# Tree attention on one core: three stores and three layings moved in GpSimd's program, and K of heads 32 to 47 read in rows of sixteen nodes

## The chip, the core and the metric

The kernel runs on one core of a Trainium2 chip. The core has a matrix engine (TensorE, called PE in the profile, with its weight loads as PEld), a vector engine (VectorE, DVE), an activation engine (ScalarE, ACT), a general engine (GpSimd, POOL) and a synchronising engine (SyncE, SP). Each works through its own list of instructions in order and waits where an instruction needs something that is not there yet. Sixteen DMA engines move data between the memory outside (HBM) and the memory on the core (SBUF). Matrix products are written to a third memory, PSUM.

The metric is the device time of one execution in microseconds. The kernel before takes 132.79 us, the median of 3 runs that lay between 132.54 and 132.94.

## The reference

Q, K and V hold 8 x 12 = 96 heads with 512 nodes of 64 numbers each, in float32. The 512 nodes are a binary tree in heap order: the parent of node i is (i - 1) // 2. A node attends to itself and its ancestors only.

```python
mask[i, i] = 1
parent = i
while parent > 0:
    parent = (parent - 1) // 2
    mask[i, parent] = 1
...
scores = np.einsum('bhqd,bhkd->bhqk', Q, K) * scale
scores = scores + (1 - mask) * (-1e9)
weights = np.exp(scores - np.max(scores, axis=-1, keepdims=True))
weights = weights / (np.sum(weights, axis=-1, keepdims=True) + 1e-10)
return np.einsum('bhqk,bhkd->bhqd', weights, V).astype(np.float32)
```

## The kernel before

**Work.** The 96 heads are worked through in 48 pairs. A loop over i from 0 to 48 holds, at step i, some of four parts, in an order that a string of letters gives:

- S, the scores of pair i. `scores1` multiplies the top 128 nodes of the tree, as keys, with all queries; `scores2` does the rest. Both first multiply two small code matrices (`codes`, `far`), whose product is a large negative number wherever the mask forbids. ACT takes the exponential out of PSUM (tile `s`) into SBUF (tile `e`).
- V, the products of pair i - 1: `values` multiplies `e` with the values `vt` into the PSUM tile `ob`, and `norm` lets DVE take the reciprocal of the sums (`rec`, line 733) and scale the result into the output tile `of` (line 735). There is one `ob`, so the next pair's V waits for this scaling.
- K and Q, a turn of keys or queries of later pairs. They lie in SBUF with nodes on the partitions, and PE transposes them into PSUM (`ktp`, `qtp`), from where DVE copies them to where the scores read them (`kq` or `kk` for keys, `qq` for queries). One turn covers two pairs.

**Three layouts.** A load puts 4, 8 or 16 neighbouring nodes of a head in one row of a partition, so a row read from HBM is 1, 2 or 4 KB long (the load converts float32 to bf16 on its way). Pairs below `WIDE` = 8 have rows of four nodes. Queries of pairs from `FAR` = 16 on have rows of sixteen, keys only from `KFAR` = 24 on. In a turn of keys, `wide_k` (rows of eight) has three DVE copies into `kq`, lines 482, 486 and 490, and serves its own two pairs. `far_k` (rows of sixteen) has three copies into `kk`, two at line 521 and one at 525; the turns work on groups of four pairs, and only both turns together complete the keys of their group. So the keys of pairs 16 to 19 are then needed whole before S of pair 16.

**Lists of values.** V needs its values in three tiles `vt`, which there are twice; 16 heads share one set. POOL, DVE and ACT copy pieces of the loaded rows `vst` there (line 374). Which piece goes to which engine at which step is a fixed table (`BY_VECTOR`, `BY_SCALAR`, `STEADY_VECTOR`, and POOL's own program). DVE's last piece for heads 32 to 47, called C0, is copied at step 16, and V of pair 16 (at step 17) needs it.

**POOL's program.** `pool_program` is one list, in the order in which POOL works through it. It holds nearly every load and store (issuing one takes POOL 0.6 to 0.95 us), POOL's pieces of the values (`spread_top`: four pieces of 16 heads' top nodes; `spread_pool`: named pieces) and four copies `lay_beside` (line 448). A laying copies a loaded tile of the last sixteen heads so that the two heads of a pair lie beside each other, and the turns of the pairs 40 to 47 read that copy. POOL works strictly in this order. Before it issues a load or store it waits until the one eight places earlier in its queue has landed, so eight are under way at most. All of them go through one queue (q0 in the profile), in order of issue.

**The order around the change.** Up to head 55 the loads stand in a written list. From head 56 on a loop over blocks of eight heads appends: K, Q, what remains of V, and a store of eight heads as soon as it lies `BEHIND` = 56 heads behind the load. The remaining stores follow, with the layings between them. Stores of the last heads go through the queues of SP and ACT.

```python
WIDE, FAR, KFAR = 8, 16, 24
...
if i >= max(FAR, KFAR - 4):
    steps = ("SVK", "SVQ", "SVK", "SQV")[i % 4]
elif i == FAR - 1:
    steps = "SQVK"
```

Of the kernel before, what the change touches and what calls it, by code (L numbers as in the profile page):

```python
# [10 lines left out]
CODE = 2048.0  # L11
CODE_ROWS = 40
NOUT = 20
BEHIND = 56

# [104 lines left out]
def kernel(  # L120
# [7 lines left out]
    nc = tc.nc  # L128
# [4 lines left out]
    NH = B * H  # L133
    NQ = NH // 4
    NP = 2 * NQ
    WIDE, FAR, KFAR = 8, 16, 24
    KB, VB = 8, 16
    assert NH % VB == 0

# [611 lines left out]
    APART, APART_AT, APART_ROWS = 72, 38, 116  # L751
# [7 lines left out]
    def pool_program():  # L759

        ops = [
            (load_k, 2, 2), (load_q, 2, 2), (load_v, 0, 4), (load_v, 4, 4),
            (load_k, 4, 2), (load_k, 6, 2), (load_q, 4, 2), (load_k, 8, 4),
            (load_q, 6, 2), (load_q, 8, 4), (load_v, 8, 8), (load_k, 12, 4),
            (load_q, 12, 4), (load_k, 16, 4), (load_rows, 1, "upper"),
            (load_q, 16, 4), (load_rows, 1, "even"), (load_k, 20, 4), (load_rows, 1, "odd"),
            (load_q, 20, 4), (load_k, 24, 8), (load_q, 24, 4), (load_rows, 2, "upper"),
            (load_q, 28, 4), (load_rows, 2, "leaves0", "leaves1"), (load_k, 32, 8), (load_q, 32, 8),
            (load_rows, 3, "upper"),
            (spread_pool, (1, "Z0", 8, 16), (1, "Z1", 8, 16), (1, 6, 8, 16), (1, 9, 8, 16)),  # L770
            (load_q, 40, 8), (load_k, 40, 8), (load_rows, 3, "leaves0", "leaves1"), (load_k, 48, 8),
            (spread_top, 2), (spread_pool, (2, "Z0", 0, 16), (2, "Z1", 0, 16)), (load_q, 48, 8),
            (spread_pool, (2, "X", 0, 16), (2, "M", 0, 16), (2, "D1", 0, 16)), (spread_top, 3, 0, 12),
            (load_rows, 4, "upper"), (spread_top, 3, 12, 16),
        ]
        loaded, stored = 72, 0
        for h in range(56, NH, KB):
            top = [(spread_top, h // VB + 0)] if h % VB == 8 and 4 <= h // VB + 0 < NH // VB else []
            if top:
                top.append((spread_pool, (h // VB, "Z0", 0, 16), (h // VB, "Z1", 0, 16)))  # L780
            ops += [(load_k, h, KB)] + top + [(load_q, h, KB)]
            if h == 64:
                ops.append((
                    spread_pool, *[(3, part, 0, 16) for part in ("Z0", "Z1", "X", "M", "D1")]
                ))
            while loaded < min(h + 32, NH):
                names = ("leaves0", "leaves1") if loaded % VB else ("upper",)
                ops.append((load_rows, loaded // VB) + names)
                loaded += KB
            if top:  # L790
                o = h // VB
                ops.append((spread_pool, *[(o, part, 0, 16) for part in ("X", "M", "D1")]))
# [4 lines left out]
        while stored < NH - KB:  # L797
            n = 2 if stored == APART else 0
            ops.append((store, nc.gpsimd, stored + n, KB - n))
            if stored == 40:  # L800
                ops.append((lay_beside, "qst", 80 // KB))
            if stored == 64:
                ops += [(lay_beside, "kst", 88 // KB), (lay_beside, "qst", 88 // KB)]
            stored += KB
        ops += [(store, nc.gpsimd, NH - KB + h, 2) for h in (0, 4)]
        return ops

# [165 lines left out]
```

## Time and profile before

| | |
|---|---|
| median of 3 runs | 132.79 us (132.54 to 132.94) |
| the profiled execution's own time | 132.49 us |
| its span, from first to last instruction | 130.7 us |
| busy share of the span | PE 87%, DVE 81%, ACT 77%, POOL 65% |
| granted TensorE clock, mean | 0.986 of full speed |
| read from HBM, written to it | 37.94 MB, 12.58 MB |

The profiled execution is 0.30 us below the median and lies 1.8 us above its span. Times of the trace are counted from the start of the span. A row of the timeline names the start, the busy time, engine, line, operation and tiles with the number of instructions that it merges, and in square brackets how long the engine had been idle before, and what ended that. Issue rows (DMA_DIRECT2D) are the time that POOL spends on issuing, not the transfer's. The figure GB/s counts bytes on the side that is written; a load reads float32 and writes bf16, so it reads twice that from HBM.

### The profile page before, as it was taken

Reading aid. Unit: us, or ns where it says so; the run is one execution under the profiler, and the core shown is the slowest. Engines: PE = TensorE matmul, PEld = TensorE weight load, DVE = VectorE, ACT = ScalarE, POOL = GpSimd, SP = SyncE. Lnnn points to the kernel's source line nnn. Section 1 sums busy time; section 2 is a strip of 40 time slices with the busy share of each in tenths; the row PEclk is TensorE's granted clock in tenths of the full one; section 3 lists DMA queues with packets and bytes.
Section 4 is the critical chain, followed back from the end, with each engine's and each line's share of the span. In section 5 each row is a group of like instructions: output and inputs, shape, how many; then the busy total and the mean of one; then the engine's idle time right before and its main releaser. Section 6 shows DMA issues by size and latency. Waiting matters only on the chain.

```text
span 130.7 us, 5436 instructions
## 1 busy us (share of the span) xinstructions
PE 113.7 (87%) x2353; PEld 81.0 (62%) x2353; DVE 105.6 (81%) x254; ACT 101.1 (77%) x163; POOL 84.4 (65%) x116
## 2 busy tenths in 40 slices
PE   6688969999799887899998999896999997999940
PEld 2354755766577566677776786674677675776630
DVE  3349779888999998989998998987898997894560
ACT  4179676989779995968987799797689785889930
POOL 6999625354483999995299899953999963202130
PEclk9999999999999999999999999999999999999995
DMA  2999999999999999999999999999999999999984
GB/s 89 248 190 192 201 195 201 201 202 205 201 203 208 208 205 207 208 210 205 207 211 201 283 292 210 270 309 231 338 228 322 257 277 397 402 404 386 382 339 145
DMA packets 26071, 32.25 MB, mean 247 GB/s; under 512 B 1240, under 2 KB 19544, under 8 KB 26048
## 3 DMA queue, kind: packets, MB, share of 16 engines
q0 software_dynamic: 24384, 30.41, 111.4%
q1 hardware_dynamic: 944, 0.91, 2.2%
q10 hardware_dynamic: 720, 0.59, 1.5%
q8 instruction: 18, 0.29, 0.8%
q14 instruction: 5, 0.04, 0.1%
HBM read 37.94 MB, written 12.58 MB: 386 GB/s over the span
## 4 chain that ended last, share of the span: by engine, by line
DVE 29%; DMA 28%; PE 22%; POOL 7%; ACT 6%; issue 4%; ACTq 0%; DVEq 0%; POOLq 0%
DMA vst<-in_V_dram 17%; DMA qst<-in_Q_dram 11%; DVE of L735 9%; PE ob L696 8%; DVE vt L374 6%; PE s L601 3%; DVE qq L577 3%; ACT e L652 3%; DVE rec L733 3%; DVE kk L521 3%; POOL kst L247 2%; PE s L608 2%; DVE kk L525 2%; POOL qst L247 2%; ACT e L618 2%
## 5 line engine op out<-in xcount | busy, mean ns | idle before, releaser
L618 ACT ACTIVATE e<-s 128x1024 bf16<-128x1024 f32 x40 | 40.9, 1024 | 15.0 <-PE s L608 14.6
L696 PE MATMUL ob<-vt,e 128*128 128x65 bf16 (+1 forms) x940 | 37.1, 197 | 2.6 <-DVE of L735 1.0
L696 PEld LDWEIGHTS <-e 128*128 128x128 bf16 (+1 forms) x960 | 30.1, 102 | 9.6 <-DVE of L735 1.9
L374 POOL COPY vt<-vst 32x512 int32<-32x512 int32 (+4 forms) x44 | 32.5, 739 | 4.7 <-PE ob L696 2.5
L652 ACT ACTIVATE e<-s 128x384 bf16<-128x384 f32 x80 | 34.7, 490 | 0.0
L735 DVE TENSOR_TENSOR of<-ob,rec 128x512 f32<-128x512 f32 x47 | 32.5, 691 | 1.6
L374 DVE COPY vt<-vst 32x1024 bf16<-32x1024 bf16 (+5 forms) x47 | 20.9, 445 | 2.8 <-DMA vst<-in_V_dram 1.9
L743 POOL DMA_DIRECT2D out_dram<-of x13 | 11.5, 888 | 12.9 <-DVE of L735 12.4
L733 DVE RECIPROCAL rec<-ob 128x8 f32<-128x8 f32 x47 | 9.5, 202 | 9.9 <-PE ob L696 9.3
L257 POOL DMA_DIRECT2D kst<-in_K_dram x11 | 8.0, 725 | 7.4 <-DMA qst<-in_Q_dram 3.2
L601 PE MATMUL s<-far,codes 40*128 40x512 bf16 x64 | 12.5, 386 | 0.0
L635 PEld LDWEIGHTS <-codes 40*128 40x128 bf16 x80 | 6.2, 94 | 8.7 <-issue 3.9
L614 ACT ACTIVATE e<-s 128x1024 bf16<-128x1024 f32 x8 | 8.2, 1023 | 4.1 <-PE s L608 4.0
L577 DVE COPY qq<-qtp 128x1024 bf16<-128x1024 bf16 x16 | 10.9, 680 | 0.3 <-PE qtp L572 0.3
L635 PE MATMUL s<-far,codes 40*128 40x384 bf16 x64 | 10.7, 324 | 0.4 <-ACT e L652 0.2
L257 POOL DMA_DIRECT2D qst<-in_Q_dram x12 | 8.5, 708 | 3.8 <-DMA vst<-in_V_dram 1.9
L374 ACT COPY vt<-vst 32x512 int32<-32x512 int32 (+3 forms) x19 | 10.4, 545 | 0.4
L608 PE MATMUL s<-qq,kk 64*128 64x512 bf16 x48 | 9.2, 378 | 1.0 <-DVE qq L577 1.0
L646 PEld LDWEIGHTS <-kk 64*128 64x128 bf16 x192 | 8.4, 94 | 2.6
L521 DVE COPY kk<-ktp 128x256 bf16<-128x256 bf16 x24 | 9.0, 414 | 0.7 <-PE ktp L513 0.7
L302 POOL DMA_DIRECT2D vst<-in_V_dram x7 | 5.6, 800 | 6.0 <-DMA vst<-in_V_dram 4.3
L572 PE MATMUL qtp<-ptile,qst 128*64 128x128 bf16 x192 | 7.5, 221 | 1.7 <-DVE qq L577 1.0
(64 smaller groups left out, 178.2 us busy)
## 6 DMA issues: line engine op xcount, KB each, us to landing
out_dram<-of POOLq DMA_DIRECT2D x10, 1024.0 KB, 15.2
kst<-in_K_dram POOLq DMA_DIRECT2D x9, 512.0 KB, 16.5
qst<-in_Q_dram POOLq DMA_DIRECT2D x8, 512.0 KB, 14.8
vst<-in_V_dram POOLq DMA_DIRECT2D x12, 256.0 KB, 13.5
vst<-in_V_dram POOLq DMA_DIRECT2D x6, 512.0 KB, 12.9
qst<-in_Q_dram POOLq DMA_DIRECT2D x6, 256.0 KB, 12.1
kst<-in_K_dram POOLq DMA_DIRECT2D x4, 256.0 KB, 10.3
out_dram<-of POOLq DMA_DIRECT2D x1, 768.0 KB, 13.0
```

The source lines that it names most:

```text
L257: return nc.gpsimd.dma_start(out=kept[b][:, h0 % KB:h0 % KB + n, :, :].rearrange("p (g x) t d -> p g (x t d)", x=x), in_=src[:, h0 // x:(h ...
L374: return copy(out=dst, in_=src)
L521: nc.vector.tensor_copy(out=columns(flat, 32 * unit, (640, 4), (step, 2), (4, 8), (1, 4)), in_=columns(kp, base, (256, 4), (128, 2), (1, 8 ...
L577: nc.vector.tensor_copy(out=qqs[j][:, :, 8 * last:8 * last + 8, :].rearrange("p b u c -> p b (u c)"), in_=quarters,)
L601: nc.tensor.matmul(out=sp[:, a, :], lhsT=(k1code if i < WIDE else k1wide)[64 * a:64 * a + CODE_ROWS, :], rhs=(q1code, q1wide, q1far)[(i >= ...
L608: nc.tensor.matmul(out=sp[:, a, :], lhsT=keys(i, a, TOP), rhs=qTs[i][64 * a:64 * a + 64, :, :].rearrange("p t c -> p (t c)"), start=False, ...
L618: ) if i < WIDE else nc.scalar.activation(
L635: nc.tensor.matmul(out=flat[:, a, :, :].rearrange("p u (t c) -> p u t c", t=4)[:, :, :, 32 // n:], lhsT=k2wide[64 * a:64 * a + CODE_ROWS, ...
L652: nc.scalar.activation(out=e2s[i % NE][:, a, :, 32:128].rearrange("p t (r u) -> p t r u", u=n), in_=flat[:, a, :, :].rearrange("p u (t r) ...
L696: nc.tensor.matmul(out=ob[lo:hi, a, 65 * t:65 * t + 65], lhsT=e[:, a, PLACE[t], lo:hi], rhs=vt[vtile[tile_v][0]][:, head(i, a) % VB, vtile ...
L733: nc.vector.reciprocal(out=rec[:, a:a + n, :, :], in_=o4[:, a:a + n, :, D:D + 1])
L735: nc.vector.tensor_tensor(out=ofs[j][:, h0:h1 + 1:head(i, 1) - head(i, 0), :, :], in0=o4[:, a:a + n, :, 0:D], in1=rec[:, a:a + n, :, :].to ...
```

## The change

**POOL's program from head 56 on is written out.** Read against the order before:

- the stores of heads 8 to 15, 16 to 23 and 24 to 31 each stand behind one more block of loads. Before, they stood ahead of K of heads 72, 80 and 88; now they stand behind Q of these heads and, for 72 and 88, behind the pieces of values that go with that block;
- the load of V's upper rows for heads 80 to 95 stands behind K and Q of heads 64 to 71 and the pieces that follow them, where it stood ahead of the first store;
- the layings: Q of heads 80 to 87 is laid right after K of these heads, ahead of the stores of heads 24 and 32 (it stood behind the stores of heads 32 and 40); K and Q of heads 88 to 95 are laid ahead of the stores of heads 40 to 71 (they stood behind them).

POOL's queue before, from the load of V's leaf rows for heads 80 to 95 (`vst`, 32x8x512) to Q of heads 80 to 87; `kst` and `qst` are loads of K and Q, `out_dram` is a store, each of eight heads:

```order
L293 DMA vst<-in_V_dram 32x8x512 x2
L743 DMA out_dram<-of 128x8x256
L257 DMA kst<-in_K_dram 128x2x1024
L374 COPY vt_0_115<-vst 32x16x32 x4
L374 COPY vt_1_116<-vst 32x32x32 x2
L257 DMA qst<-in_Q_dram 128x2x1024
L374 COPY vt_2_117<-vst 32x32x32 x2
L374 COPY vt_1_116<-vst 32x8x2x32
L743 DMA out_dram<-of 128x8x256
L257 DMA kst<-in_K_dram 128x2x1024
L257 DMA qst<-in_Q_dram 128x2x1024
```

The same place now:

```order
L292 DMA vst<-in_V_dram 32x8x512 x2
L301 DMA vst<-in_V_dram 64x16x256
L256 DMA kst<-in_K_dram 128x2x1024
L373 COPY vt_0_115<-vst 32x16x32 x4
L373 COPY vt_1_116<-vst 32x32x32 x2
L256 DMA qst<-in_Q_dram 128x2x1024
L373 COPY vt_2_117<-vst 32x32x32 x2
L373 COPY vt_1_116<-vst 32x8x2x32
L742 DMA out_dram<-of 128x8x256
L256 DMA kst<-in_K_dram 128x2x1024
L256 DMA qst<-in_Q_dram 128x2x1024
```

The store that stood ahead of K of heads 72 to 79 (the first `kst` here), that of heads 8 to 15, is now behind the pieces that follow Q of these heads; the upper rows of V (`vst`, 64x16x256) have come in ahead of that K.

POOL's queue before, from the last pieces of values to the end of the layings (L448, `kst<-kst` and `qst<-qst`):

```order
L374 COPY vt_1_122<-vst 32x8x2x32
L448 COPY kst<-kst 128x1024
L743 DMA out_dram<-of 128x8x256 x2
L448 COPY qst<-qst 128x1024
L743 DMA out_dram<-of 128x8x256 x3
L448 COPY kst<-kst 128x1024
L448 COPY qst<-qst 128x1024
L743 DMA out_dram<-of 128x6x256
```

The same place now:

```order
L373 COPY vt_1_122<-vst 32x8x2x32
L447 COPY kst<-kst 128x1024
L447 COPY qst<-qst 128x1024
L742 DMA out_dram<-of 128x8x256 x2
L447 COPY kst<-kst 128x1024
L447 COPY qst<-qst 128x1024
L742 DMA out_dram<-of 128x8x256 x4
L742 DMA out_dram<-of 128x6x256
```

The layings have moved ahead of stores; the first laying stands where it stood, right behind the last pieces.

**K of heads 32 to 47 in rows of sixteen nodes.** `KFAR` falls from 24 to 16, so the keys of pairs 16 to 23 are loaded and turned as those from pair 24 on were: two loads of eight heads change their shape, and four turns become `far_k`. The turns of keys move to even steps (14, 16, 18) where they stood on 15, 17 and 19, those of queries to odd ones; with that, K of heads 40 to 47 is loaded ahead of Q of these heads.

DVE's queue before, from the copies of the keys' turn at step 15 (`kq`) on; `rec` and `of` are the two operations of a pair's scaling, `qq` a turn of queries, `vt_2_123` and `vt_1_116` pieces of values:

```order
L482 COPY kq<-ktp 128x2x128
L486 COPY kq<-ktp 128x4x64
L490 COPY kq<-ktp 128x4x2x64
L374 COPY vt_2_117<-vst 32x8x2x64
L733 RECIPROCAL rec<-ob 128x8
L735 TENSOR_TENSOR of<-ob,rec 128x2x256
L577 COPY qq<-qtp 128x4x256
L374 COPY vt_1_116<-vst 32x8x2x64
L733 RECIPROCAL rec<-ob 128x8
L735 TENSOR_TENSOR of<-ob,rec 128x2x256
L482 COPY kq<-ktp 128x2x128
```

The same place now, from the queries' turn at step 15 (`qq`) on:

```order
L576 COPY qq<-qtp 128x4x256
L732 RECIPROCAL rec<-ob 128x8
L734 TENSOR_TENSOR of<-ob,rec 128x2x256
L373 COPY vt_2_117<-vst 32x8x2x64
L732 RECIPROCAL rec<-ob 128x8
L734 TENSOR_TENSOR of<-ob,rec 128x2x256
L520 COPY kk<-ktp 128x4x2x32
L520 COPY kk<-ktp 128x8x32
L524 COPY kk<-ktp 128x8x64
L373 COPY vt_1_116<-vst 32x8x2x64
L732 RECIPROCAL rec<-ob 128x8
```

At step 16 the turn that stands between the scaling and the piece C0 (`vt_1_116`) was one of queries, with one copy; it is now one of keys, with three.

The diff:

```diff
-    WIDE, FAR, KFAR = 8, 16, 24
+    WIDE, FAR, KFAR = 8, 16, 16
...
-            (load_q, 40, 8), (load_k, 40, 8), (load_rows, 3, "leaves0", "leaves1"), (load_k, 48, 8),
+            (load_k, 40, 8), (load_q, 40, 8), (load_rows, 3, "leaves0", "leaves1"), (load_k, 48, 8),
...
-            if stored + KB + BEHIND <= h + KB:
-                ops.append((store, nc.gpsimd, stored, KB))
-                stored += KB
-        ops.insert(-1, (lay_beside, "kst", 80 // KB))
...
+        ops += k7 + q7 + leaves(4) + out(0)
+        ops += k8 + q8 + [(spread_pool, *[(3, part, 0, 16) for part in ("Z0", "Z1", "X", "M", "D1")])]
+        ops += leaves(5) + [(load_rows, 5, "upper")]
+        ops += k9 + tops(4) + q9 + rest(4) + out(8)
+        ops += k10 + q10 + out(16)
+        ops += k11 + tops(5) + q11 + rest(5)
+        ops += [(lay_beside, "kst", 80 // KB), (lay_beside, "qst", 80 // KB)] + out(24) + out(32)
+        ops += [(lay_beside, "kst", 88 // KB), (lay_beside, "qst", 88 // KB)]
+        for h in range(40, NH - KB, KB):
+            n = 2 if h == APART else 0
+            ops += out(h + n, KB - n)
...
         if i >= max(FAR, KFAR - 4):
             steps = ("SVK", "SVQ", "SVK", "SQV")[i % 4]
+        elif i == FAR - 2:
+            steps = "SQVK"
         elif i == FAR - 1:
-            steps = "SQVK"
+            steps = "SQV"
```

In it `k8` and `q8` load K and Q of heads 64 to 71 (the digit is the block of eight heads), `tops(o)` and `rest(o)` are POOL's pieces of the sixteen heads from 16 o on, `leaves(o)` loads their leaf rows of V, and `out(h)` stores eight heads from h on.

More of the change, by code (lines that the diff above doesn't have):

```diff
@@ L13 @@
 NOUT = 20
-BEHIND = 56
 UNITS = (
@@ L775, in pool_program @@
         ]
[L776 to L792, printed above, removed]
-            if stored + KB + BEHIND <= h + KB:
-                ops.append((store, nc.gpsimd, stored, KB))
-                stored += KB
@@ L796, in pool_program, with tops @@
-        ops.insert(-1, (lay_beside, "kst", 80 // KB))
[L797 to L804, printed above, removed]
+        def tops(o):
+            return [(spread_top, o), (spread_pool, (o, "Z0", 0, 16), (o, "Z1", 0, 16))]
```

13 lines of the change are left out of this document (added).

## The prediction

> **What bounds the kernel.** I read the page first, then PE's timeline with the idle time in brackets, then POOL's, DVE's, and the windows of the end.
>
> ```profile
> PE 113.7 (87%) x2353; PEld 81.0 (62%) x2353; DVE 105.6 (81%) x254; ACT 101.1 (77%) x163; POOL 84.4 (65%) x116
> DMA  2999999999999999999999999999999999999984
> GB/s 89 248 190 192 201 195 201 201 202 205 201 203 208 208 205 207 208 210 205 207 211 201 283 292 210 270 309 231 338 228 322 257 277 397 402 404 386 382 339 145
> ```
>
> No engine is full, but the DMA engines are at 90% or more from the second slice to the 38th. The 200 GB/s of the first half are loads, 400 GB/s read; stores reach 400 at the end. So the DMA queue is a second bound beside compute, and the order within it decides when each load lands.
>
> PE, from 70 us to the end, where it stood idle:
>
> ```profile
> 70.36 0.39 PE L608 MATMUL s<-qq,kk 64*128 64x512 bf16 x2 [0.35 <-DVE qq L577]
> 80.91 0.64 PE L513 MATMUL ktp<-ptile,kst 128*64 128x128 bf16 x16 [0.23 <-DMA kst<-in_K_dram]
> 83.62 0.64 PE L572 MATMUL qtp<-ptile,qst 128*64 128x128 bf16 x16 [0.45 <-DMA qst<-in_Q_dram]
> 91.38 0.64 PE L513 MATMUL ktp<-ptile,kst 128*64 128x128 bf16 x16 [0.98 <-DMA kst<-in_K_dram]
> 93.87 0.64 PE L572 MATMUL qtp<-ptile,qst 128*64 128x128 bf16 x16 [0.23 <-DMA qst<-in_Q_dram]
> 108.66 0.39 PE L608 MATMUL s<-qq,kk 64*128 64x512 bf16 x2 [0.60 <-DVE qq L577]
> ```
>
> Four waits for loads, K and Q of heads 64 to 71 and of 72 to 79: 0.23 + 0.45 + 0.98 + 0.23 = 1.89 us. Behind 94 us no load is waited for any more, and the chain of waits runs through PE and DVE to the last scaling. The end:
>
> ```profile
> 126.55 0.42 DVE L735 TENSOR_TENSOR of<-s,rec 128x256 f32<-128x256 f32 x1
> 115.00:120.00 5.00, 4.76 (x87) 3.22 (x85) 4.01 (x9) 4.18 (x8) 0.00 (x0) 1.00 1.03 402
> 120.00:125.00 5.00, 4.81 (x104) 3.35 (x98) 2.05 (x6) 4.81 (x9) 1.87 (x3) 1.00 0.94 369
> 125.00:127.00 2.00, 0.75 (x16) 0.52 (x14) 1.76 (x5) 0.18 (x1) 0.45 (x1) 1.00 0.88 350
> 127.00:129.00 2.00, 0.00 (x0) 0.00 (x0) 0.00 (x0) 0.00 (x0) 0.00 (x0) 0.54 0.88 271
> 129.00:130.70 1.70, 0.00 (x0) 0.00 (x0) 0.00 (x0) 0.00 (x0) 0.00 (x0) 0.50 0.12 39
> ```
>
> The last number is GB/s. Compute ends at 126.97, the last bytes come some 2.4 us later, and in the last ten us the DMA engines are no longer full: 5 x 369 + 2 x 350 + 2 x 271 + 1.7 x 39 = 3,150 KB, which at the 402 of the row above take 7.8 us, where they took about 9.2 (the last window is busy for 0.2). So an earlier end of compute shortens the run one to one, up to about 1.3 us; beyond that the queue bounds it.
>
> **The moved stores and the moved load of V (a gain).** The price of a transfer in the queue: the K and Q loads that PE waited for at 91.38 and 93.87 landed 2.49 us apart, one load of eight heads. In POOL's rows the next K is there at 98.93:
>
> ```profile
> 90.23 4.87 POOL L374 COPY vt<-vst 32x512 int32<-32x512 int32 x6 [2.49 <-PE ob L696]
> 95.05 0.70 POOL L257 DMA_DIRECT2D qst<-in_Q_dram  x1
> 95.79 2.95 POOL L374 COPY vt<-vst 32x1024 int32<-32x1024 int32 x3
> 98.93 1.04 POOL L448 COPY kst<-kst 128x1024 int32<-128x1024 int32 x1 [0.19 <-DMA kst<-in_K_dram]
> 101.70 1.05 POOL L448 COPY qst<-qst 128x1024 int32<-128x1024 int32 x1
> 106.43 1.04 POOL L448 COPY kst<-kst 128x1024 int32<-128x1024 int32 x1 [0.89 <-DMA kst<-in_K_dram]
> 108.91 1.04 POOL L448 COPY qst<-qst 128x1024 int32<-128x1024 int32 x1 [1.43 <-DMA qst<-in_Q_dram]
> ```
>
> From 93.87 to 98.93 one store and that K passed: 5.06 - 2.49 = 2.57 us for a store of eight heads. K and Q of heads 64 to 71 have the upper rows of V ahead of them no more (as many bytes read as a K load: 2.5 us earlier). Those of heads 72 to 79 have these rows again, but no store of heads 8 to 15: 2.6 us earlier. Those of 80 to 87 and 88 to 95 likewise, by one store each. Each lead exceeds its wait (0.98 at most), so all four waits go: -1.89 us. Bounds: 0, if the loads land no earlier, and -1.89. I take the whole, since in the page's slices the DMA engines have no hole before 124 us. Issuing does not hold the loads back: each waits for a landing eight places earlier, and one transfer less is ahead. The stores themselves have nobody waiting but their ten output tiles, of which the first is needed again at step 40. The queue ends with one store more behind the last load; the bytes are the same.
>
> **The layings.** Those of Q 80 to 87 and of K and Q 88 to 95 now hold up the stores behind them in POOL. Laying Q 88 to 95 waits for the last load, in the worst case until 108.91 as now, so the stores of heads 40 to 71, which are now issued ahead of it, come from about 107.5 on (the load lands 2.6 us earlier). The queue holds two stores behind that load, 2 x 2.57 = 5.1 us of cover, against 1.05 for the laying and 0.9 for an issue: 0. Without that cover it would cost about 2 us. The stores of heads 74 to 95 wait for DVE as before. Laying Q 80 to 87 directly behind K ends a short wait of PE, 0.2 us in the list of waits:
>
> ```profile
> PEld L566 <- POOL qst L448: 0.2, 1, 0.2
> 100.49 0.61 PE L507 MATMUL ktp<-ptile,kst 128*128 128x128 bf16 x8
> ```
>
> **What is late next.** The second row is PE's turn on the first laid K. It needs POOL's laying, which stands behind nine pieces and a load that start only when V of pair 31 frees `vt` (90.23, released by PE's `ob`). From there POOL needs 98.93 + 1.04 - 90.23 = 9.74 us, less its own 0.19 for the load: 9.55. PE took 100.49 - 90.23 = 10.26 us, of which 0.98 + 0.23 were the last two waits: 9.05. With these gone PE arrives half a us before the laying: +0.50. Bounds 0 (POOL's pieces run quicker) and 0.7; so -1.89 becomes, with the 0.2, -1.59.
>
> **Rows of sixteen for K of heads 32 to 47 (a cost).** DVE's groups, with the mean time of one in ns as the second number behind the bar:
>
> ```profile
> L374 DVE COPY vt<-vst 32x1024 bf16<-32x1024 bf16 x28 | 14.1, 504 | 1.1 <-DMA vst<-in_V_dram 0.6
> L577 DVE COPY qq<-qtp 128x1024 bf16<-128x1024 bf16 x16 | 10.9, 680 | 0.3 <-PE qtp L572 0.3
> L521 DVE COPY kk<-ktp 128x256 bf16<-128x256 bf16 x24 | 9.0, 414 | 0.7 <-PE ktp L513 0.7
> L525 DVE COPY kk<-ktp 128x512 bf16<-128x512 bf16 x12 | 8.1, 679 | 0.0
> L482 DVE COPY kq<-ktp 128x256 bf16<-128x256 bf16 x8 | 3.3, 415 | 0.3 <-PE ktp L473 0.3
> L486 DVE COPY kq<-ktp 128x256 bf16<-128x256 bf16 x8 | 3.3, 414 | 0.0
> L490 DVE COPY kq<-ktp 128x512 bf16<-128x512 bf16 x8 | 3.3, 412 | 0.0
> ```
>
> A far turn is 2 x 0.414 + 0.679 = 1.51 us, a wide one 1.24: 0.27 more, four times, 1.06 us. PE's side costs nothing: sixteen transposes either way. Where these turns lie, between 45 and 62 us, DVE is almost never idle:
>
> ```profile
> 50.39 0.69 DVE L577 COPY qq<-qtp 128x1024 bf16<-128x1024 bf16 x1 [0.28 <-PE qtp L572]
> 55.22 0.51 DVE L374 COPY vt<-vst 32x1024 bf16<-32x1024 bf16 x1
> 55.79 0.29 PE L696 MATMUL ob<-vt,e 128*64 128x65 bf16 x7 [0.37 <-DVE vt L374]
> 56.12 0.21 DVE L733 RECIPROCAL rec<-ob 128x8 f32<-128x8 f32 x1 [0.38 <-PE ob L696]
> 60.30 0.21 DVE L733 RECIPROCAL rec<-ob 128x8 f32<-128x8 f32 x1 [0.26 <-PE ob L696]
> ```
>
> Its idle time there is 0.28 + 0.38 + 0.26 = 0.92. If all of it were filled, 1.06 - 0.92 = 0.14 would remain. On the other side the piece C0, which ends at 55.73 and for which PE waits at 55.79, now stands behind a turn of keys instead of one of queries, 1.51 - 0.68 = 0.83 later; were that never made up, 1.06 + 0.83 = 1.9. I take 1.1: DVE's work sets the pace here and the postponed queries are work that falls away later, but the idle times are PE's chain from V to scaling, which remains. The turn of keys on even steps itself costs nothing more: at step 15 PE's two turns become one, and at step 14 it has two. Loading K of 40 to 47 ahead of Q brings each one place nearer to its new turn: 0.
>
> The two loads in longer rows: the page's GB/s go from 195 to 205 in slices 5 to 12, where rows of four and eight nodes pass, to 205 to 211 in slices 13 to 21 with many rows of sixteen. That is at most 5% of 2 x 2.49, 0.25 us of queue. Since the end hangs on compute, I count 0.
>
> **Sum.** -1.89 (waits) + 0.50 (laying late) - 0.2 (Q laid in time) + 1.1 (keys) = -0.49 us. The profiled execution, 132.49, becomes 132.0; the median of the runs is 0.30 above it, so 132.3. No change means within 0.3%, 0.4 us.
>
> **Rivals.** *The far turns hide* in DVE's idle time (0.14 instead of 1.1): the sum is -1.45, of which the queue lets 1.3 through: 131.5. For it speaks that DVE idles as much as the turns add; against it, that each idle piece ends with a wait for PE, which itself had waited for DVE.
>
> *The far turns lengthen the chain* and end on the other side: C0 late, then S of pair 20 behind its queries, which the new order turns one step ahead (PE's rows at 70.36 and 108.66 show 0.35 and 0.60 lost in just this place of the four-step pattern). 1.9 + 0.35 = 2.25 gives -1.59 + 2.25 = +0.66: 133.4. It decides from 1.6 on; by 2.0 the run is measurably slower.
>
> *The loads land no earlier* than before, because POOL issues them too late. Then the 1.1 of the keys only eats into the 1.89 of waiting, and the time stays at 132.8. Against it the page's list of issues, with the median time to landing in us:
>
> ```profile
> qst<-in_Q_dram POOLq DMA_DIRECT2D x8, 512.0 KB, 14.8
> ```
>
> POOL is some six transfers ahead of what lands.
>
> *POOL's copies against DVE's.* A piece of values takes DVE 0.42 alone and up to 1.06 beside POOL's copies:
>
> ```profile
> 43.13 4.82 POOL L374 COPY vt<-vst 32x512 int32<-32x512 int32 x6
> 47.16 1.06 DVE L374 COPY vt<-vst 32x1024 bf16<-32x1024 bf16 x1
> 49.69 0.42 DVE L374 COPY vt<-vst 32x1024 bf16<-32x1024 bf16 x1
> ```
>
> The layings now follow one another more closely beside the last pieces of heads 80 to 95 (at 103 and 105). Two pieces that are each 0.64 longer give -0.49 + 1.28 = +0.8, 133.6. Against it: over all 28 pieces of this shape the mean is 0.50, so most are hardly disturbed. [...]
>
> **Chances.** Forecast 0.38; far turns hidden 0.20; far turns on the chain 0.20; loads no earlier 0.14; POOL against DVE 0.08. The forecast stands at -0.49 with some 0.4 to either side from the bounds of the keys and of the laying, so it is about half in faster and half in no change. Faster: 0.21 + 0.20 = 0.41; no change: 0.17 + 0.14 + 0.02 = 0.33; slower: 0.26. The likeliest alone: 131.9 to 132.7. The range takes in the hidden turns and most of the lengthened chain: 131.5 to 133.4.
>
> **What would show it.** Right: no wait of PE for `kst` or `qst` between 78 and 96 us; DVE's copies into `kk` up from 24 and 12 to 32 and 16, those into `kq` down from 8 to 4 in each of the three groups; PE waiting up to 0.5 us for POOL's first laying near 100; DMA at 90% until 120. The second products of S of pair 24, at 70.36 now, about 1.1 later. Wrong: PE's waits for loads still there (no earlier landing); those of pair 24 beyond 72 us (chain); a hole in the DMA row near 108 (layings).

## The result and the profile after

The changed kernel takes 135.96 us, the median of six executions between 133.82 and 136.32; the kernel before, six times beside it, took 132.77. The ratio is 1.0111, with an interval of 1.0069 to 1.0153: about 1.1% slower, where half a microsecond of gain was forecast. The six executions lie in two groups (133.8 and 134.7, and four from 135.9 to 136.3); this ratio and those below rest on the lower group of a kernel's executions, the medians on all of them, and since the profile below is of one at 135.9, that of the same kernel run again, at 134.53, is read beside it.

The head of the page of after, and the row of its DMA engines:

```profile
span 134.1 us, 5434 instructions
PE 114.1 (85%) x2350; PEld 81.1 (60%) x2353; DVE 108.0 (81%) x254; ACT 101.1 (75%) x163; POOL 84.1 (63%) x116
DMA  3999999999999999999999999999999897999983
```

The span is 3.4 us longer. DVE has 2.4 us more of work, where 1.1 were forecast, and in the DMA row there are now slices at 80 and 70% before the end.

Where PE stood idle for 0.2 us or more after 46 us:

```profile
48.03 0.64 PE L571 MATMUL qtp<-ptile,qst 128*64 128x128 bf16 x16 [1.52 <-DMA qst<-in_Q_dram]
53.29 0.39 PE L607 MATMUL s<-qq,kk 64*128 64x512 bf16 x2 [0.92 <-DVE qq L576]
57.66 0.29 PE L695 MATMUL ob<-vt,e 128*64 128x65 bf16 x7 [0.77 <-DVE vt L373]
63.23 0.39 PE L607 MATMUL s<-qq,kk 64*128 64x512 bf16 x2 [0.21 <-DVE qq L576]
68.86 0.79 PE L695 MATMUL ob<-vt,e 128*128 128x65 bf16 x20 [0.53 <-DVE of L734]
81.88 0.39 PE L607 MATMUL s<-qq,kk 64*128 64x512 bf16 x2 [0.38 <-DVE qq L576]
87.47 0.79 PE L695 MATMUL ob<-vt,e 128*128 128x65 bf16 x20 [0.50 <-DVE of L734]
100.70 0.39 PE L607 MATMUL s<-qq,kk 64*128 64x512 bf16 x2 [0.21 <-DVE qq L576]
106.52 0.79 PE L695 MATMUL ob<-vt,e 128*64 128x65 bf16 x20 [0.54 <-DVE of L734]
```

Between 78 and 96 us no load is waited for any more. In the place of those 1.89 us stand two waits for DVE, 0.38 and 0.50. And between 46 and 58 us, where the keys' turns were moved, there are three waits of 3.2 us together; the first is for a load. Before, PE stood idle there for 1.56 us, in waits of 0.21, of 0.37 and of 0.98, so the growth is 1.65. The largest of these three, which the prediction does not have:

```profile
49.71 0.64 PE L572 MATMUL qtp<-ptile,qst 128*64 128x128 bf16 x16 [0.98 <-DVE qq L577]
```

How late the work runs is read from DVE's scalings (`of`). Before, those of pairs 12 and 23:

```profile
45.45 0.69 DVE L735 TENSOR_TENSOR of<-ob,rec 128x512 f32<-128x512 f32 x1
72.27 0.69 DVE L735 TENSOR_TENSOR of<-ob,rec 128x512 f32<-128x512 f32 x1
```

After, the same two, and the last one of all:

```profile
45.44 0.69 DVE L734 TENSOR_TENSOR of<-ob,rec 128x512 f32<-128x512 f32 x1
74.64 0.69 DVE L734 TENSOR_TENSOR of<-ob,rec 128x512 f32<-128x512 f32 x1
128.28 0.42 DVE L734 TENSOR_TENSOR of<-s,rec 128x256 f32<-128x256 f32 x1
```

Level at pair 12, 2.37 us late at pair 23, and 128.28 - 126.55 = 1.73 late at the end. The row that the prediction named, the second products of S of pair 24, comes 2.37 later than the 70.36 of before, where 1.1 were forecast; it lies beyond the 72 that were to tell of the lengthened chain:

```profile
72.73 0.39 PE L607 MATMUL s<-qq,kk 64*128 64x512 bf16 x2
```

The remaining 1.7 of the 3.4 us lie behind compute: the last scaling ends 134.1 - 128.70 = 5.4 us before the end of the span, where it was 130.7 - 126.97 = 3.7. This "drain", from the end of the last scaling to the end of the span, serves below to tell the two bounds apart. No kernel of this study drained in less than 3.7 us; where it is 3.7, compute is taken to have set the end, and what is over that is put down to the queue.

The windows of after in which the DMA engines (the last but one column) had holes, and its end; the last column is GB/s:

```profile
104.00:106.00 2.00, 1.98 (x42) 1.39 (x34) 1.92 (x5) 1.72 (x4) 2.00 (x3) 1.00 0.82 246
110.00:112.00 2.00, 1.78 (x37) 1.21 (x35) 1.14 (x3) 1.31 (x3) 1.88 (x3) 1.00 0.78 169
125.00:130.00 5.00, 2.28 (x52) 1.73 (x49) 2.47 (x7) 1.88 (x4) 1.42 (x2) 0.97 0.93 346
130.00:132.00 2.00, 0.00 (x0) 0.00 (x0) 0.00 (x0) 0.00 (x0) 0.00 (x0) 0.50 0.64 187
```

Before, the first two had none:

```profile
104.00:106.00 2.00, 2.00 (x44) 1.53 (x42) 1.94 (x4) 1.79 (x3) 1.54 (x2) 1.00 1.12 219
110.00:112.00 2.00, 2.00 (x46) 1.58 (x43) 1.64 (x5) 1.56 (x4) 0.44 (x1) 1.00 0.99 383
```

The same kernel run again (134.53 us, span 132.8) ends otherwise. DVE's rows there, a piece of values and the last scaling:

```profile
104.11 1.74 DVE L373 COPY vt<-vst 32x1024 bf16<-32x1024 bf16 x1
128.62 0.42 DVE L734 TENSOR_TENSOR of<-s,rec 128x256 f32<-128x256 f32 x1
```

It drains in 132.8 - 129.04 = 3.8 us, so there the whole loss of 2.1 us is compute's (128.62 - 126.55 = 2.07). A piece of values that takes 0.42 us undisturbed took 1.74.

### The profile page after: what moved, and what is told of

Same layout as the page of the kernel before. It is cut to its first block, busy times and chain, and to the rows that moved or that the text cites. A ratio compares the mean times of both kernels' runs of the same rounds, so it can differ in the third digit from the quotient of the medians.

```text
span 134.1 us, 5434 instructions
## 1 busy us (share of the span) xinstructions
PE 114.1 (85%) x2350; PEld 81.1 (60%) x2353; DVE 108.0 (81%) x254; ACT 101.1 (75%) x163; POOL 84.1 (63%) x116
## 4 chain that ended last, share of the span: by engine, by line
DVE 40%; DMA 24%; PE 22%; issue 4%; ACT 4%; POOL 2%; ACTq 0%; POOLq 0%
DVE of L734 13%; DMA qst<-in_Q_dram 11%; PE ob L695 9%; DMA kst<-in_K_dram 7%; DVE vt L373 6%; DVE kk L520 6%; DVE kk L524 5%; DVE qq L576 5%; DMA vst<-in_V_dram 5%; DVE rec L732 4%; PE s L600 3%; ACT e L651 2%; PE s L607 2%; ACT e L617 1%; PE ktp L506 1%
## 5 line engine op out<-in xcount | busy, mean ns | idle before, releaser
L373 DVE COPY vt<-vst 32x1024 bf16<-32x1024 bf16 (+5 forms) x47 | 22.5, 479 | 3.4 <-DMA vst<-in_V_dram 2.5
L607 PE MATMUL s<-qq,kk 64*128 64x512 bf16 x64 | 12.3, 378 | 2.1 <-DVE qq L576 1.7
L645 PEld LDWEIGHTS <-kk 64*128 64x128 bf16 x256 | 11.2, 94 | 3.5
L520 DVE COPY kk<-ktp 128x256 bf16<-128x256 bf16 x32 | 11.9, 415 | 0.0
L645 PE MATMUL s<-qq,kk 64*128 64x160 bf16 (+1 forms) x256 | 11.8, 208 | 0.0
L524 DVE COPY kk<-ktp 128x512 bf16<-128x512 bf16 x16 | 10.9, 681 | 0.0
```

Of the source, the lines that this page charges most:

```text
L373: return copy(out=dst, in_=src)
L520: nc.vector.tensor_copy(out=columns(flat, 32 * unit, (640, 4), (step, 2), (4, 8), (1, 4)), in_=columns(kp, base, (256, 4), (128, 2), (1, 8 ...
L524: nc.vector.tensor_copy(out=columns(flat, 128 * last, (320, 8), (32, 2), (2, 16), (1, 2)), in_=columns(kp, 16, (128, 8), (32, 2), (1, 16), ...
L645: nc.tensor.matmul(out=flat[:, a, :, lo:hi], lhsT=keys(i, a, WTILE2[t]), rhs=qT[64 * a:64 * a + 64, :, lo:hi], start=False, stop=t == 1, s ...
```

## The experiments

The theory at the start was that of the prediction with its keys dearer. The rivals were the queue's holes from the layings, POOL against DVE, and that the queue, not compute, takes what the earlier loads bring. All kernels in one table; "end" is the end of the last scaling in the profile, "vt" the time of DVE's 47 pieces of values in all forms, a row of the page:

| kernel | ratio to before (95%) | median, us | end | span | drain | vt |
|---|---|---|---|---|---|---|
| before | 1 | 132.77 | 126.97 | 130.7 | 3.7 | 20.9 |
| changed | 1.0111 (1.0069 to 1.0153) | 135.96 | 128.70 | 134.1 | 5.4 | 22.5 |
| changed again (e11) | 1.011 (1.0059 to 1.016) | 134.71 | 129.04 | 132.8 | 3.8 | 23.4 |
| POOL's program alone (e2) | 1.0005 (0.9979 to 1.0031) | 133.05 | 124.44 | 131.2 | 6.8 | 20.2 |
| keys alone (e1) | 1.0048 (1.0015 to 1.0081) | 133.69 | 129.14 | 132.9 | 3.8 | 23.9 |
| e2 less a store (e7) | 0.9846 (0.9805 to 0.9887) | 130.87 | 125.68 | 129.4 | 3.7 | 21.7 |
| before less a store (e8) | 0.9945 (0.9921 to 0.9968) | 132.19 | 126.82 | 130.5 | 3.7 | 21.8 |
| even steps alone (e5) | 0.9995 (0.9958 to 1.0031) | 133.03 | 129.91 | 133.6 | 3.7 | 23.9 |
| rows of sixteen alone (e6) | 1.0035 (0.999 to 1.008) | 134.11 | 127.59 | 131.3 | 3.7 | 20.9 |
| changed, Q last in step 14 (e4) | 1.019 (1.0133 to 1.0246) | 135.40 | 130.46 | 134.7 | 4.2 | 23.7 |
| changed, layings back (e3) | 1.0168 (1.0122 to 1.0213) | 135.37 | 130.28 | 134.0 | 3.7 | 22.8 |
| e2, last layings back (e9) | 1.0021 (0.9996 to 1.0045) | 133.18 | 125.79 | 131.3 | 5.5 | 21.7 |
| changed, last layings back (e10) | 1.0112 (1.0066 to 1.0158) | 134.41 | 128.21 | 132.7 | 4.5 | 23.5 |
| changed less a store (e12) | 1.0078 (1.0033 to 1.0122) | 134.66 | 128.86 | 132.8 | 3.9 | 23.9 |

The profiles of e1, e3, e4 and e5 hold a stretch at half clock (last section), which is in their end and span.

### POOL's program alone, and the keys alone

The first run is the changed kernel with the keys as before:

```diff
-    WIDE, FAR, KFAR = 8, 16, 16
+    WIDE, FAR, KFAR = 8, 16, 24
...
-            (load_k, 40, 8), (load_q, 40, 8),
+            (load_q, 40, 8), (load_k, 40, 8),
...
-        elif i == FAR - 2:
-            steps = "SQVK"
         elif i == FAR - 1:
-            steps = "SQV"
+            steps = "SQVK"
```

> Only POOL's program from head 56 on as changed; keys, steps and the order of K and Q of heads 40 to 47 as before. Theory A: the four waits of PE for loads go, POOL's first laying comes half a us late, the holes are small since pair 31 is done 2.5 us earlier than in the changed kernel; 131.5 to 132.3. Theory B: the same or a little less. Theory C: holes in the queue near 104 and 112 as in the changed kernel, 134 or more.

Measured: no difference (1.0005); the median of 133.05 lies between the 132.3 of theory A and the 134 of theory C. But compute did get faster, by more than was forecast. DVE's last scaling in this kernel:

```profile
124.02 0.42 DVE L734 TENSOR_TENSOR of<-s,rec 128x256 f32<-128x256 f32 x1
```

That is 2.53 us earlier than before, and 1.5 of it come between pairs 23 and 32, where the waits for loads were (one of 0.51 is left). The span is 0.5 longer all the same. Its end in windows:

```profile
120.00:125.00 5.00, 3.02 (x62) 2.03 (x57) 2.92 (x8) 2.62 (x6) 1.43 (x2) 0.94 1.02 394
125.00:127.00 2.00, 0.00 (x0) 0.00 (x0) 0.00 (x0) 0.00 (x0) 0.00 (x0) 0.50 0.97 355
127.00:129.00 2.00, 0.00 (x0) 0.00 (x0) 0.00 (x0) 0.00 (x0) 0.00 (x0) 0.50 0.91 293
129.00:131.20 2.20, 0.00 (x0) 0.00 (x0) 0.00 (x0) 0.00 (x0) 0.00 (x0) 0.50 0.11 39
```

With all engines done by 125, the queue moves 355, 293 and 39 GB/s, almost the 350, 271 and 39 of the kernel before in the same windows. The lower rate at the end is therefore not a queue that waits for compute; the last stores run so even when nothing is waited for.

The other half is the kernel before with the three edits of the keys, and POOL's program as it was:

```diff
-    WIDE, FAR, KFAR = 8, 16, 24
+    WIDE, FAR, KFAR = 8, 16, 16
...
-            (load_q, 40, 8), (load_k, 40, 8),
+            (load_k, 40, 8), (load_q, 40, 8),
...
-        elif i == FAR - 1:
+        elif i == FAR - 2:
             steps = "SQVK"
+        elif i == FAR - 1:
+            steps = "SQV"
```

> Only the keys of heads 32 to 47 in rows of sixteen, turned on even steps, with K of heads 40 to 47 loaded ahead of their Q; POOL's program from head 56 on as before. Theory A (two causes: the new turns make compute about 2 us late by pair 16, and the layings ahead of the stores leave holes in the DMA queue): compute is 2 to 2.4 us late by pair 24, the waits for K and Q of heads 64 to 79 (1.89) shrink to nothing and swallow most of it, no hole in the queue; 133.0 to 133.6. Theory B (all the loss comes from the keys, by whatever way): 134 to 136. Theory C (all the loss comes from POOL's program): 132.8, as before.

Measured 1.0048, by which 132.80 becomes 133.4, in the range of theory A. In its profile compute loses 3.28 us from pair 12 to 23 (a stretch at half clock among it), wins 1.1 back between pairs 31 and 32, and is 2.2 late at the end. That fall of 1.1 is the one that the changed kernel has there too (2.57 to 1.48): loads that land while compute is late aren't waited for, with either program. So the two halves can't be added: the lateness of the keys already eats most of the waits, and the new program has little left to save.

### Which bound ends the run

The store of heads 64 to 71 is left out of both programs, of that of the kernel with POOL's program alone (first diff) and of the one before (second):

```diff
-            ops += out(h + n, KB - n)
+            ops += out(h + n, KB - n) if h != 64 else []
```

> POOL's changed program alone, with keys and steps as before, and without the store of heads 64 to 71 (they are not written). The full one ends its compute 2.5 us earlier than before and yet takes the same time. If the DMA queue is the bound of its end, one store less shortens it by a store's 2.5 us, less what then hangs on compute: 130.4 to 131.0. If something else holds the end (the last stores of SP and ACT, or compute): 132.5 to 133.

```diff
-            ops.append((store, nc.gpsimd, stored + n, KB - n))
+            if stored != 64:
+                ops.append((store, nc.gpsimd, stored + n, KB - n))
```

> The kernel before without the same store of heads 64 to 71. No load stands behind that store. If the end of before hangs on compute, as my prediction had it: 132.3 to 132.8, as before. If queue and compute end it together, within half a us: 132.0 to 132.5. If the queue alone does: 130.5.

Measured: with the new program the store is worth 133.05 - 130.87 = 2.2 us, most of one store's 2.57; with the old one 132.86 - 132.19 = 0.7 (132.86 is the kernel before beside it). So the new program alone ends with the queue. In the kernel before the two bounds lie within 0.7 us of one another; which is the later these runs don't tell. If it is the queue, as the 0.7 us of the store suggest, a faster compute alone gains nothing; if it is compute, as the drain of 3.7 suggests, it gains those 0.7 at most. The one kernel that did speed compute up, POOL's program alone, gained nothing.

### What of the keys costs

Three kernels take the edits of the keys apart. The even steps and the order of the loads alone, with rows of eight as before:

```diff
-            (load_q, 40, 8), (load_k, 40, 8),
+            (load_k, 40, 8), (load_q, 40, 8),
...
-        if i >= max(FAR, KFAR - 4):
+        if i >= FAR:
...
-        elif i == FAR - 1:
+        elif i == FAR - 2:
             steps = "SQVK"
+        elif i == FAR - 1:
+            steps = "SQV"
```

> POOL's program as before, keys of heads 32 to 47 in rows of eight as before, but turned on even steps (14, 16, 18) and loaded ahead of their queries for heads 40 to 47, as in the changed kernel. The run with the keys alone was 2.69 us behind at the scaling of pair 23. If the order of the turns causes most of this: 1.6 to 2.2 us behind here, 133.2. If the longer copies cause most: 0.8 us behind or less, 132.8, as before.

Rows of sixteen alone, with the turns on the steps of before:

```diff
-    WIDE, FAR, KFAR = 8, 16, 24
+    WIDE, FAR, KFAR = 8, 16, 16
...
-        if i >= max(FAR, KFAR - 4):
+        if i >= 20:
```

> The complement: keys of heads 32 to 47 in rows of sixteen, turned on the steps of before (15, 17, 19), loads in the order of before, POOL's program as before. If the order causes most of the 2.69: about 1.0 us behind at pair 23 (four turns by 0.27), 132.8 to 133.1. If the longer copies do: 1.6 or more, 133.3. A third way: the keys of pair 16 are now needed whole one step later than they are turned, which may cost a wait of its own of about 1 us.

And the changed kernel with Q as the last part of step 14:

```diff
         elif i == FAR - 2:
-            steps = "SQVK"
+            steps = "SVKQ"
```

> The changed kernel, but step 14 takes V and K ahead of its turn of queries (S, V, K, Q instead of S, Q, V, K), so that PE does not wait 1.5 us for the load of Q of heads 32 to 39 with V and K behind it. Theory A with the wait as the larger part of the 2 us: pair 16 comes 0.7 to 1.3 us earlier than in the changed kernel and the run is shorter by about 1 us. Rival (DVE's longer turns are the larger part): less than 0.4 us.

Measured, as the growth of the lateness from pair 12 to pair 23 in the profiles: even steps alone +1.1, rows alone +2.6, both together +2.4 in the changed kernel and again +2.4 when it was run again, and +1.7, +2.1 and +3.0 in the kernels e3, e10 and e12, which have the same keys and steps. POOL's program alone has -0.5 and the two kernels less a store +0.2 and +0.5, so the scatter is some 0.5 to 0.7 either way. PE's waits show the pieces. Even steps alone:

```profile
48.22 0.64 PE L572 MATMUL qtp<-ptile,qst 128*64 128x128 bf16 x16 [0.38 <-DMA qst<-in_Q_dram]
53.18 0.39 PE L608 MATMUL s<-qq,kq 64*128 64x512 bf16 x2 [0.62 <-DVE qq L577]
57.52 0.29 PE L696 MATMUL ob<-vt,e 128*64 128x65 bf16 x7 [0.73 <-DVE vt L374]
```

These are the three places of the changed kernel, with smaller numbers: Q of heads 32 to 39 is now turned ahead of V and K of its step and its load isn't there; S of pair 16 waits for the queries turned just before it; and V of pair 16 for the piece C0. The forecast had put this order at nothing. The growth of 1.1 is too small a measure of it, though. This profile was already 1.36 us late at pair 12, behind its stretch at half clock, and who comes late waits less for a load that lands at the same time (48.22 here, 48.03 in the changed kernel). At pair 23 the even steps alone are 2.47 late, as late as both together (2.37). How late an execution without that stretch would be isn't shown; and by the ratio, 0.9995, the even steps alone cost nothing at the end of the run.

The wait for Q is not the whole price either. In e10 that load happened to land at 46.73 and PE waited 0.38 for it, but then 1.33 for `qq` at 52.42, where the changed kernel has 1.52 and 0.92: what one wait loses the next takes.

Rows of sixteen alone:

```profile
52.27 0.39 PE L608 MATMUL s<-qq,kk 64*128 64x512 bf16 x2 [1.52 <-DVE kk L525]
62.70 0.39 PE L608 MATMUL s<-qq,kk 64*128 64x512 bf16 x2 [1.52 <-DVE kk L525]
```

On the old steps the second far turn of a group stands just ahead of the scores that need the group whole, and PE waits for the last of its three copies, 1.52 us, twice: the third way of its expectation. So these rows cost waits with either order of the steps, and by the ratios (1.0035 here, 1.0048 for the keys alone, intervals that overlap) neither order is shown to be the better. With Q last the wait only changes its place:

```profile
45.29 0.64 PE L512 MATMUL ktp<-ptile,kst 128*64 128x128 bf16 x16 [0.89 <-DMA kst<-in_K_dram]
50.93 0.64 PE L571 MATMUL qtp<-ptile,qst 128*64 128x128 bf16 x16 [1.54 <-DVE qq L576]
```

PE's 1.54 there is for DVE's `qq`, and instead of a gain of about 1 us the ratio is 1.019, the highest of all, with an interval that overlaps that of the changed kernel.

The second piece of the cost is in the column "vt". DVE's group of pieces, all forms, before (time, then mean ns behind the bar):

```profile
L374 DVE COPY vt<-vst 32x1024 bf16<-32x1024 bf16 (+5 forms) x47 | 20.9, 445 | 2.8 <-DMA vst<-in_V_dram 1.9
```

Rows of sixteen alone, on the old steps:

```profile
L374 DVE COPY vt<-vst 32x1024 bf16<-32x1024 bf16 (+5 forms) x47 | 20.9, 445 | 2.5 <-DMA vst<-in_V_dram 1.6
```

Even steps alone:

```profile
L374 DVE COPY vt<-vst 32x1024 bf16<-32x1024 bf16 (+5 forms) x47 | 23.9, 508 | 3.3 <-DMA vst<-in_V_dram 2.4
```

The six kernels with the old steps spend 20.2 to 21.8 us on these 47 copies, the eight with the new ones 22.5 to 23.9, though the copies are the same. The mean goes from 21.2 to 23.5: 2.3 us of DVE's time, twice the 1.06 that the rows of sixteen add. What lies beside the long ones is seen best in the changed kernel run again. POOL's rows around the piece of 104.11 to 105.85:

```profile
102.72 1.79 POOL L742 DMA_DIRECT2D out_dram<-of  x2
104.51 1.05 POOL L447 COPY kst<-kst 128x1024 int32<-128x1024 int32 x1
```

and PE's wait behind it:

```profile
106.86 0.79 PE L695 MATMUL ob<-vt,e 128*64 128x65 bf16 x20 [1.57 <-DVE of L734]
```

The piece begins while POOL issues stores and ends 0.29 us after the laying that follows (105.56): its 1.74 us lie over the last 0.40 us of the issues and the whole 1.05 of the laying, and PE then stood 1.57 us. In the profile of the first execution the piece there took 0.70 and PE waited 0.54. The other long pieces lie beside POOL's work too. Call a piece long that takes over 0.06 us more than the quickest of its shape: in the profiles of before and of the changed kernel's first execution every long piece overlaps a copy or an issue of POOL. Before, 13 are long, by 3.4 us together, of which 2.1 fall on those beside copies; in the changed kernel 15, by 5.0 and 3.7, and run again 15, by 5.8 and 4.3. So what the new steps add lies beside POOL's copies. Yet lying there is not enough, since 24 of the other 34 pieces of before overlap POOL's work as well and take no longer, and no kernel was run without POOL's copies; as the cause they are argued from this, not shown by a run.

### The layings

All layings back behind their stores:

```diff
-        ops += [(lay_beside, "kst", 80 // KB), (lay_beside, "qst", 80 // KB)] + out(24) + out(32)
-        ops += [(lay_beside, "kst", 88 // KB), (lay_beside, "qst", 88 // KB)]
+        ops += [(lay_beside, "kst", 80 // KB)] + out(24) + out(32)
...
+            if h == 40:
+                ops.append((lay_beside, "qst", 80 // KB))
+            if h == 64:
+                ops += [(lay_beside, "kst", 88 // KB), (lay_beside, "qst", 88 // KB)]
```

> The changed kernel, but the layings stand among the stores as before (Q of heads 80 to 87 behind the stores of heads 24 to 47, K and Q of heads 88 to 95 behind the stores up to head 71). Theory A: the DMA engines have no hole behind 100 us, the end follows compute, which is 1.7 us later than before; 134.0 to 134.6 against 135.9 of the changed kernel's profile. Rival (the holes cost nothing, the end follows something else): as the changed kernel, 135 to 136.

Measured 1.0168, no better than the changed kernel (the intervals overlap). By its profile PE now waits for the laying of Q of heads 80 to 87:

```profile
106.30 0.62 PE L565 MATMUL qtp<-ptile,qst 128*128 128x128 bf16 x8 [1.58 <-POOL qst L447]
```

Three stores stand ahead of this laying here, where the kernel before has two; the keys alone, in the order of before, have 0.54 at this wait. So the run shows the price of a late laying, and does not decide about the holes. The two last ones alone, back behind the store of heads 64 to 71, in POOL's program alone (e9) and in the changed kernel (e10); the edit is the same:

```diff
-        ops += [(lay_beside, "kst", 88 // KB), (lay_beside, "qst", 88 // KB)]
...
+            if h == 64:
+                ops += [(lay_beside, "kst", 88 // KB), (lay_beside, "qst", 88 // KB)]
```

> POOL's changed program alone (keys and steps as before), with the layings of K and Q of heads 88 to 95 back behind the store of heads 64 to 71; the layings of heads 80 to 87 stay ahead of the stores. In the run with the whole program these last two layings waited 2.3 and 1.4 us for PE to free their tiles, and the store behind them was issued at 107.5. If that hole in the queue is what ate the gain: the queue runs through, compute ends about 2.5 us earlier than before, and the run takes 132.1 to 132.5, bound by the queue. If the hole costs nothing: as the whole program, 133.0.

> The changed kernel with the same two layings back behind the store of heads 64 to 71. Theory: of the two holes in its DMA queue (near 104 and 111) the second goes, compute stays 1.7 to 2.5 us late, PE does not wait for the first laying of queries as it did when all layings went back; 134.0 to 134.6. Rival (the holes don't set the end): as the changed kernel, 135 to 136.

Measured: no difference in either, 1.0021 against 1.0005 and 1.0112 against 1.0111. In e10 the hole at 110 to 112 is gone (share 1.01 for 0.78), and the ratio stays. So that hole, which may stand behind the longer drain of the first profile, isn't what makes the changed kernel 1.1% slower.

### The changed kernel again, and with one store less

The changed kernel is run once more without any edit, for a second profile.

> The changed kernel once more, for its spread (133.8 to 136.3 so far, where before lay between 132.4 and 134.1). If the spread comes from how late compute is when it reaches the loads and layings, a shorter run shows compute further ahead at pair 23 and a later or shorter hole in the queue at 110 to 114; if it comes from the clock or the queue's rate, the steps agree and the rates differ.

The result is told above: 1.011 again, all of it compute in this profile. Compute is 0.65 us less late at pair 23 than in the first profile (1.72 against 2.37), but it was 0.64 ahead at pair 12 already; the hole at 110 to 112 is smaller (share 0.91 for 0.78). Then it is run without the store of heads 64 to 71:

```diff
-            ops += out(h + n, KB - n)
+            ops += out(h + n, KB - n) if h != 64 else []
```

> The changed kernel without the store of heads 64 to 71 (they are not written), as was done with the kernel before (0.6 us shorter) and with POOL's program alone (2.2 us shorter). If the changed kernel's end hangs on its late compute: 133.7 to 134.5, at most half a us under the full one's 134.3 to 134.7. If the holes in its queue set the end: some 2 us shorter, 132.3 to 132.9. If sometimes the one and sometimes the other: the long runs of 136 are gone and the short ones stay, spread under 1 us.

Measured 1.0078 against 1.011, some 0.4 us, with intervals that overlap; its nine executions lie between 133.38 and 136.21, so the spread is no smaller. Its window before the last stores:

```profile
120.00:125.00 5.00, 4.77 (x92) 3.23 (x93) 2.11 (x7) 4.83 (x9) 0.89 (x1) 1.00 0.55 206
```

The DMA engines are at 55% there, while PE is busy for 4.77 of the 5 us. A queue that is this free makes the kernel hardly faster: the changed kernel ends with its late compute.

## Why the prediction was wrong

**The end (wrong).** The step "an earlier end of compute shortens the run one to one, up to about 1.3 us" fails. It took the falling GB/s of the last windows for a queue that waits. POOL's program alone ended compute 2.53 us earlier for nothing, with the same falling rates, and a store less is worth only 0.7 us in the kernel before. The room was 0.7 at most, and the one kernel that tried it found none, so there was not room for the 1.3 that the rival of the hidden turns was let through with, and none is shown for the forecast's 0.49.

**The moved stores and V (right in its place, not in the sum).** In the changed kernel all four waits for loads are gone, as forecast. Alone the program has 1.5 us less between pairs 23 and 32: the wait of 0.51 that is left there is for Q of heads 72 to 79, which landed 93.87 - 91.60 = 2.27 us earlier, near the forecast 2.6, while PE came earlier too. But in the changed kernel only 0.9 of it shows (2.37 late at pair 23, 1.48 at pair 32), since PE now waits there for DVE, 0.38 and 0.50 us; and with the keys alone, under the old program, about as much falls away. The prediction added -1.89 and the keys' cost as if they were independent. Its rival "the loads land no earlier" held this thought, that a late compute eats the waits; it belonged into the sum itself.

**The keys (mis-sized, the main error).** Forecast +1.1, measured +2.4 by pair 23, somewhat over the rival with the longer chain (2.25). The size of the turns was right, as DVE's groups in the profile of after show:

```profile
L520 DVE COPY kk<-ktp 128x256 bf16<-128x256 bf16 x32 | 11.9, 415 | 0.0
L524 DVE COPY kk<-ktp 128x512 bf16<-128x512 bf16 x16 | 10.9, 681 | 0.0
```

They are 32 and 16 copies, at 415 and 681 ns where 414 and 679 were forecast. What failed is "the turn of keys on even steps itself costs nothing more": alone it cost at least 1.1 us by pair 23, and lengthened the pieces of values. C0 did come late, but that wait grew by 0.4 only (0.37 to 0.77); the larger part was two waits that the prediction had not listed, 1.52 for the load of Q and 0.92 for `qq` of pair 16, in the place of the 0.98 and 0.21 of before. The "0" for the order of the loads speaks of heads 40 to 47 and is not what failed: the load that PE waits for is Q of heads 32 to 39, which stands in the queue where it stood, but whose turn at step 14 now comes ahead of V.

**POOL against DVE (a rival at 0.08, and seen).** It was looked for at the two layings and priced at 1.28, two pieces of 1.06 for 0.42. The pieces there took 1.04 and 0.70 in the first profile, and 1.03 and 1.74 in the second, with PE's wait of 1.57; long pieces were there in a smaller size all along the run, where the new steps put 2.3 us more on the 47 pieces.

**The layings (place right, price open).** The first laying is not waited for by PE in the changed kernel, where compute arrives late, nor with POOL's program alone, where compute is early: PE begins its turn there at 98.36, right behind the end of the laying at 98.30, since POOL came to it 1.67 us sooner (97.26 for 98.93). So the forecast half microsecond did not show in either. "Cover 5.1 us, cost 0" is wrong for the first profile, which has holes at 104 to 106 and 110 to 112 and 1.7 us more drain, and holds for the second (drain 3.8); taking the second hole away changed no ratio.

**The sum.** Compute, in the changed kernel run again: -0.6 at pair 12, +2.35 to pair 23, -0.9 to pair 32, +1.7 to pair 36 with the long piece, -0.5 to the end; together 2.07, and the end followed it. What stays open: the changed kernel is slower than the keys alone by 1.011 against 1.0048, with intervals that overlap, and whether that rests on the long pieces beside the layings or on the queue's holes differs from one profile to the other.

No version of this study that stores all heads beats the kernel before; POOL's program alone (1.0005) and the even steps alone (0.9995) equal it.

## What to carry to other kernels

Before a gain is summed up, ask which bound takes over, and test it: leaving one late transfer out of the kernel tells in one run (0.7 or 2.2 us here) what the GB/s of the last windows could not. A cost and a wait on the same chain are not added, since lateness ahead of a wait is paid out of that wait first (1.1 us of it with the keys alone here). A turn that is moved by a step with the same work is not free where it stands, even if other waits hide it by the end of the run (0.9995 here): list when its operands' loads land there, what its copies wait for, and whether the pieces beside them grow longer (23.5 us for 21.2 here).

## What was not expected of the hardware

**A stretch at half clock behind a short wait.** The profile of the keys alone holds one. A wait of PE there:

```profile
52.42 0.39 PE L608 MATMUL s<-qq,kk 64*128 64x512 bf16 x2 [1.27 <-DVE qq L577]
```

and the windows around it; the last but two column is the granted clock:

```profile
50.00:53.80 3.80, 2.44 (x54) 1.77 (x52) 3.67 (x7) 1.95 (x4) 3.51 (x7) 1.00 1.13 208
53.80:57.20 3.40, 3.40 (x51) 2.43 (x50) 2.75 (x7) 2.05 (x5) 3.18 (x8) 0.50 1.20 210
```

In the window with this wait PE was busy 2.44 of 3.80 us at full clock; in the next 3.4 us the clock was 0.50. The kernel before has 3.80 of 3.80 busy in the first of these windows and no dip. The kernel with Q last had one of some 6.8 us in the same place, from 52.49 on, after the wait of 1.54 (a mean clock of 0.83 at 50 to 53.8, 0.50 to 57.2 and 0.62 to 60). But the two profiles of the changed kernel have waits of 1.52 and 0.92, and of 1.42 and 0.81, in this place and no dip, and dips occurred where nothing had been edited yet (even steps alone, 0.50 at 22 to 25.4 us; changed with layings back, 0.57 at 13 to 17). So these waits alone don't bring a dip, and they are not its only cause; what does is not shown.

**A long piece beside issues alone.** The kernel before has one without a laying beside it. DVE's piece:

```profile
104.90 0.89 DVE L374 COPY vt<-vst 32x1024 bf16<-32x1024 bf16 x1
```

and what POOL did at that time, until 105.54:

```profile
102.68 2.86 POOL L743 DMA_DIRECT2D out_dram<-of  x3
```

The next laying starts at 106.43 only. The piece took 0.47 longer than the 0.42 of an undisturbed one and ended 0.25 after the issues. It is not so beside each issue: the piece at 102.89, beside the first of these three, took 0.42. Over the whole trace of before, the long pieces beside issues alone are 6, by 1.3 us together, where those beside copies are 7, by 2.1: a piece can be long beside POOL's issues as well as beside its copies.
